# Eight experts on one core: the last two results in one tile, and one more weight tile loaded in halves

## The chip, the cores and the metric

The kernel runs on one core of a Trainium2 chip. The metric is the device time of one execution in microseconds (us), the median of three runs. The profile is that of one further execution; its span starts at the first and ends at the last recorded instruction, and is shorter than the device time by some 1.8 us.

## The reference

There are 8 experts. Each takes 256 tokens of width 512 through a hidden layer of width 2048 with ReLU and back. All inputs and the result are float32.

```python
# x (8,256,512)  w1 (8,512,2048)  w2 (8,2048,512)  b1 (8,2048)  b2 (8,512)
h = np.matmul(x, w1) + b1[:, np.newaxis, :]
h = np.maximum(h, 0)
out = (np.matmul(h, w2) + b2[:, np.newaxis, :]).astype(np.float32)
```

w1 and w2 of one expert are 4 MB each in float32, so 64 MB of weights are read for 4 MB of input and 4 MB of results.

## The kernel before

**Stages.** For every expert there are two products. The first (`first_product`, L114) makes hT, the hidden layer with the 2048 hidden units on partitions, in 16 blocks of 128 units (j), each of 4 matmuls over the input width (kc) followed by one ScalarE instruction that adds the bias, takes the ReLU and writes fp16 (L128). The second (`second_product`, L166) makes the result for two blocks of 128 tokens (tb) in the PSUM tiles po0 and po1: one matmul with a row of ones for the bias b2 (L171), then 16 matmuls over j (L178) for each tb. The inputs are turned by VectorE in 32x32 blocks (`transposes`, L95).

**Order.** The loop at L227 runs over steps s = 0 to 10. Step s does the first product of expert s and then the second product of expert s - 3 (LAG = 3), so steps 8, 9 and 10 have the second products of experts 5, 6 and 7 alone. Nearly all transfers are issued by GpSimd in an order written out by hand, the `ring` list (L215 to L225), and kept so by `ordered`. GpSimd's loads also turn float32 in memory into fp16 in the tile. The ring ends with w2 of expert 7, then the two flushes (L138), which store the results of the groups of experts. A load can be issued only when the buffer that it overwrites has been used up; w1 and w2 have three buffers each.

**w2 in halves.** `load_w2` (L88) loads the w2 of the experts in HALVED (6 and 7) as two transfers, j = 0 to 7 and j = 8 to 15. For these experts `second_product` does both token blocks with the first half of j and then both with the second (L174 to L177), so that it can start when half of the tile has landed. For the others po0 is finished before po1 is begun, and all of w2 is needed at the start.

**Results.** `store` (L142) copies po0 by VectorE (L156) and po1 by ScalarE (L157) to SBUF. Experts 0 to 3 share one tile and so do experts 4 and 5 (GROUPS, L36): with n experts to a tile, an expert takes 128 / n partitions, and a partition holds 2n consecutive tokens of one expert, which are 4n KB in one piece in the result. Each po tile is then copied in n pieces of 128 / n partitions. hT's tokens are put in a matching order by L128 (`split`). A group's tile is stored by its flush, on GpSimd's queue. Experts 6 and 7 are in no group: each has a tile of its own from out_pool with rows of 4 KB, stored at once by L164. Expert 6's goes out in three pieces (PARTS, L40): rows 0 to 24 and 121 to 127 by SyncE and rows 25 to 120 by ScalarE. Expert 7's goes out in one piece of 128 rows by SyncE.

Of the DMA queues in the profile, q0 is that of GpSimd's transfers, q1 that of SyncE's and q10 that of ScalarE's; q8 loads instructions.

Of the kernel before, what the change touches and what calls it, by code (L numbers as in the profile page):

```python
# [10 lines left out]
def kernel(  # L11
# [9 lines left out]
    nc = tc.nc  # L21
    fp32 = mybir.dt.float32
    fp16 = mybir.dt.float16
    E, T, H = x.shape
    M = w1.shape[2]
    P = 128
    nTB = T // P
# [4 lines left out]
    LAG = 3  # L32

    GROUPS = {0: 4, 4: 2}  # L36
    HALVED = (E - 2, E - 1)


    PARTS = {E - 2: ((0, 25, False), (25, 121, True), (121, 128, False))}  # L40
    nXF32 = 2
    X_LOADS = {2: 2, 4: 4}

    def ordered(ins):
        return tc.keep_in_program_order(ins)
# [7 lines left out]
    group_pool = ctx.enter_context(tc.tile_pool(name="groups", bufs=1))  # L53
    out_pool = ctx.enter_context(tc.tile_pool(name="outp", bufs=2))
# [13 lines left out]
    pending = {}  # L68
    results = {}
    group_of = {first + i: (first, n) for first, n in GROUPS.items() for i in range(n)}  # L70

# [16 lines left out]
    def load_w2(e):  # L88
        src = w2[e].rearrange("(p j) h -> p j h", j=nJ)
        w2_sb[e] = w2_pool.tile([P, nJ, H], fp16, tag="w2", name="w2sb")  # L90
        half = nJ // 2 if e in HALVED else nJ
        for lo in range(0, nJ, half):
            ordered(nc.gpsimd.dma_start(out=w2_sb[e][:, lo : lo + half], in_=src[:, lo : lo + half]))  # L93

    def transposes(e):  # L95


        t, p0, R = x16[e]
        n = R // nTB
        xT[e] = xT_pool.tile([P, nKC, T], fp16, tag="xT", name="xT")  # L100
        for g in range(T // R // B):
            src = t[p0 + B * g : p0 + B * (g + 1)]
            for b in range(nB):
                block = src[:, :, b * (H // nB) : (b + 1) * (H // nB)].rearrange(
                    "p (n tb) (i kc) -> p tb kc n i", tb=nTB, kc=nKC)
                out = xT[e][b * B : (b + 1) * B].rearrange(
                    "p kc (tb g i n) -> p tb g kc n i", tb=nTB, i=B, n=n)
                if n == 1:
                    nc.vector.transpose(out=out[:, :, g, :, 0, :], in_=block[:, :, :, 0, :])  # L109
                    continue  # L110
                for tb in range(nTB):
                    nc.vector.transpose(out=out[:, tb, g], in_=block[:, tb])  # L112

    def first_product(e):  # L114
        hT[e] = hT_pool.tile([P, nJ, T], fp16, tag="hT", name="hT")
        split = group_of[e][1] if e in group_of else 1
        for j in range(nJ):
            bias_at = j * B + e * nB + nB - 1
            ph = psum_h.tile([P, T], fp32, tag="ph", name="ph")
            for kc in range(nKC):  # L120
                ordered(nc.tensor.matmul(  # L121
                    out=ph,
                    lhsT=w1_sb[e][:, kc, :].rearrange("p (q j) -> p q j", j=nJ)[:, :, j],
                    rhs=xT[e][:, kc, :],
                    start=(kc == 0),
                    stop=(kc == nKC - 1),
                ))
            nc.scalar.activation(  # L128
                out=hT[e][:, j, :].rearrange("p (tb k i) -> p tb k i", tb=nTB, k=split),
                in_=ph.rearrange("p (tb i k) -> p tb k i", tb=nTB, k=split),  # L130
                func=mybir.ActivationFunctionType.Relu,
                bias=b1T[:, bias_at : bias_at + 1],
                scale=1.0,
            )
            if j == nJ // 2 and e + 1 < E:
                transposes(e + 1)
# [3 lines left out]
        ordered(nc.gpsimd.dma_start(out=dst, in_=src))  # L140

    def store(e, po):  # L142
        if e in group_of:
            first, n = group_of[e]
            split, rows = n, P // n
            if e == first:
                results[e] = group_pool.tile(
                    [P, split * nTB, H], fp32, tag=f"out{e}", name=f"out{e}")
        else:
            first, n, split, rows = e, 1, 1, P  # L150
            results[e] = out_pool.tile([P, nTB, H], fp32, tag="out", name="out")
        out_sb = results[first]
        at = (e - first) * rows
        for k in range(split):
            part = slice(k * rows, (k + 1) * rows)
            nc.vector.tensor_copy(out=out_sb[at : at + rows, k * nTB, :], in_=po[0][part])  # L156
            nc.scalar.copy(out=out_sb[at : at + rows, k * nTB + 1, :], in_=po[1][part])  # L157
        dst = out[first : first + n].rearrange("e (p r) h -> (e p) r h", r=split * nTB)
        if e in group_of:
            if e == first + n - 1:  # L160
                pending[first] = (dst, out_sb)
            return
        for p0, p1, scalar in PARTS.get(e, ((0, P, False),)):
            (nc.scalar if scalar else nc.sync).dma_start(out=dst[p0:p1], in_=out_sb[p0:p1])  # L164

    def second_product(e):  # L166
        po = []
        for tb in range(nTB):
            t = psum_o.tile([P, H], fp32, tag=f"po{tb}", name=f"po{tb}")
            po.append(t)  # L170
            ordered(nc.tensor.matmul(  # L171
                out=t, lhsT=ones1, rhs=b2_sb[0:1, e * H : (e + 1) * H], start=True, stop=False,
            ))
        half = nJ // 2 if e in HALVED else nJ  # L174
        for lo in range(0, nJ, half):
            for tb in range(nTB):
                for j in range(lo, lo + half):  # L177
                    ordered(nc.tensor.matmul(  # L178
                        out=po[tb],
                        lhsT=hT[e][:, j, tb * P : (tb + 1) * P],  # L180
                        rhs=w2_sb[e][:, j, :],
                        start=False,
                        stop=(j == nJ - 1),
                    ))
        store(e, po)

    x32 = []
    for e in range(nXF32):
# [4 lines left out]
        out=b2_sb,  # L193
        in_=b2.rearrange("e h -> (e h)").rearrange("(o f) -> o f", o=1),
# [12 lines left out]
    for b in range(nB):  # L207
        nc.vector.transpose(  # L208
            out=b1T[b * B : (b + 1) * B, nB - 1 - b : nB - 1 - b + nJ * B],
            in_=b1_rows.rearrange("r (i j) -> r j i", j=nJ),  # L210
# [4 lines left out]
    ring = []  # L215
# [6 lines left out]
            ring.append((s - 2, load_w2, (s - LAG,)))  # L222
    ring.append((E + LAG - 3, load_w2, (E - 1,)))
    for first, n in GROUPS.items():
        ring.append((first + n + LAG, flush, (first,)))  # L225

    for s in range(E + LAG):  # L227
        while ring and ring[0][0] <= s:
            _, put, args = ring.pop(0)
            put(*args)  # L230
        if s < E:
            first_product(s)
        if s >= LAG:
            second_product(s - LAG)
# [31 lines left out]
```

## Time and profile before

| what | value |
|---|---|
| device time | 181.51 us (181.47 to 181.75, 3 runs) |
| span of the profiled execution | 179.7 us |
| busy: PE, PEld, DVE, ACT, POOL | 129.1, 85.8, 88.0, 70.2, 13.1 us |
| DMA: GpSimd's queue (q0) | 3232 packets, 38.35 MB, 96.6% of 16 engines |
| DMA: SyncE's queue (q1) | 476 packets, 1.70 MB, 2.4% |
| DMA: ScalarE's queue (q10) | 112 packets, 0.39 MB, 0.5% |
| DMA: instructions (q8) | 6 packets, 0.10 MB, 0.2% |
| HBM | 71.39 MB read, 4.19 MB written |
| copy of a po tile, 64 or 128 partitions | DVE 0.69 us, ACT 0.58 to 0.59 us |
| half of w2 (1024 KB), issue to landing | 16.9 to 30.9 us |
| last store (512 KB), issue to landing | 4.8 us |

PE is the tensor engine's matmuls and PEld its weight loads, DVE is VectorE, ACT ScalarE and POOL GpSimd. In the slices each digit stands for a fortieth of the span, 4.5 us, in tenths. The queue's share is the summed time of its packets as a share of 16 DMA engines over the whole span; packets of one engine overlap a little, so shares can come out above 1 in a stretch. A transfer's time to landing runs from its issue, so for transfers that stand in a queue it is mostly waiting.

### The profile page before, as it was taken

Reading aid. Unit: us, or ns where it says so; the run is one execution under the profiler, and the core shown is the slowest. Engines: PE = TensorE matmul, PEld = TensorE weight load, DVE = VectorE, ACT = ScalarE, POOL = GpSimd, SP = SyncE. Lnnn points to the kernel's source line nnn. Section 1 sums busy time; section 2 is a strip of 40 time slices with the busy share of each in tenths; the row PEclk is TensorE's granted clock in tenths of the full one; section 3 lists DMA queues with packets and bytes.
Section 4 is the critical chain, followed back from the end, with each engine's and each line's share of the span. In section 5 each row is a group of like instructions: output and inputs, shape, how many; then the busy total and the mean of one; then the engine's idle time right before and its main releaser. Section 6 shows DMA issues by size and latency. Waiting matters only on the chain.

```text
span 179.7 us, 1958 instructions
## 1 busy us (share of the span) xinstructions
PE 129.1 (72%) x784; PEld 85.8 (48%) x784; DVE 88.0 (49%) x125; ACT 70.2 (39%) x151; POOL 13.1 (7%) x28
## 2 busy tenths in 40 slices
PE   0005099969595970899969597969497887999950
PEld 0004079969592320795369244844195332433420
DVE  0999942987000199999999998003200020301010
ACT  0000459969593022483099005950586020020010
POOL 7000002120201010001010001000200021010000
PEclk9999999999998798589999889999999996999996
DMA  5999999999999999999999999999999999999996
GB/s 216 251 226 199 233 212 197 233 224 193 228 230 192 221 233 215 197 230 230 204 208 230 219 193 233 226 193 222 230 215 197 233 206 204 223 212 215 335 420 250
DMA packets 3829, 40.56 MB, mean 226 GB/s; under 512 B 461, under 2 KB 477, under 8 KB 1133
## 3 DMA queue, kind: packets, MB, share of 16 engines
q0 software_dynamic: 3232, 38.35, 96.6%
q1 hardware_dynamic: 476, 1.70, 2.4%
q10 hardware_dynamic: 112, 0.39, 0.5%
q8 instruction: 6, 0.10, 0.2%
q14 instruction: 3, 0.02, 0.0%
HBM read 71.39 MB, written 4.19 MB: 421 GB/s over the span
## 4 chain that ended last, share of the span: by engine, by line
DMA 66%; PE 26%; POOL 2%; another core or an unknown queue 1%; issue 1%; ACT 0%; POOLq 0%
DMA w1sb<-in_w_dram 44%; DMA w2sb<-in_w_dram 22%; PE po L178 18%; PE ph L121 8%; PE po L171 1%; POOL w1sb L84 1%; ACT out L157 0%; POOL x L76 0%; POOL b_sb L192 0%; POOL b_rows L196 0%; POOLq L250 0%
## 5 line engine op out<-in xcount | busy, mean ns | idle before, releaser
L121 PE MATMUL ph<-xT,w1sb 128*128 128x256 f16 x512 | 63.6, 289 | 34.8 <-DMA w1sb<-in_w_dram 23.9
L121 PEld LDWEIGHTS <-w1sb 128*128 128x128 f16 x512 | 59.0, 147 | 40.3 <-DMA w1sb<-in_w_dram 32.6
L178 PE MATMUL po<-w2sb,hT 128*128 128x512 f16 x256 | 61.4, 402 | 9.4 <-DMA w2sb<-in_w_dram 9.4
L112 DVE STREAM_TRANSPOSE xT<-x 32x256 f16<-32x256 f16 (+1 forms) x64 | 53.1, 889 | 25.6 <-DMA x<-in_x_dram 18.7
L128 ACT ACTIVATE hT<-ph,b1T 128x256 f16<-128x256 f32 x128 | 56.2, 474 | 13.6 <-PE ph L121 13.4
L178 PEld LDWEIGHTS <-hT 128*128 128x128 f16 x256 | 25.9, 102 | 44.7 <-issue 19.3
L156 DVE COPY out<-po 32x512 f32<-32x512 f32 (+2 forms) x22 | 15.1, 688 | 54.0 <-PE po L178 53.8
L157 ACT COPY out<-po 32x512 f32<-32x512 f32 (+2 forms) x22 | 12.7, 579 | 69.7 <-PE po L178 69.5
L109 DVE STREAM_TRANSPOSE xT<-x 32x256 f16<-32x256 f16 x32 | 14.0, 436 | 0.5
L93 POOL DMA_DIRECT2D w2sb<-in_w_dram x10 | 5.3, 534 | 72.8 <-PE po L178 72.8
L128 ACT ACT_TABLE_LOAD x1 | 1.3, 1283 | 20.5 <-DVE b1T L208 20.5
L84 POOL DMA_DIRECT2D w1sb<-in_w_dram x8 | 4.5, 558 | 63.2 <-PE ph L121 62.4
L171 PE MATMUL po<-b_sb,ones 1*128 1x512 f16 x16 | 4.8, 379 | 0.0
L208 DVE STREAM_TRANSPOSE b1T<-b_rows 32x512 f32<-32x512 f32 x4 | 4.1, 1035 | 0.1
L201 DVE CAST x<-x 128x1024 f16<-128x1024 f32 x2 | 1.5, 757 | 3.3 <-DMA x<-in_x_dram 3.3
L140 POOL DMA_DIRECT2D out_dram<-out x2 | 1.1, 542 | 10.9 <-ACT out L157 10.9
L171 PEld LDWEIGHTS <-ones 1*128 1x128 f16 x16 | 0.9, 92 | 2.1 <-issue 2.1
L76 POOL DMA_DIRECT2D x<-in_x_dram x2 | 1.1, 552 | 0.0
L197 DVE MEMSET ones<- 1x128 f16 x1 | 0.2, 165 | 0.8 <-PEq L250 0.8
L196 POOL DMA_DIRECT2D b_rows<-in_b_dram x1 | 0.5, 515 | 0.0
L192 POOL DMA_DIRECT2D b_sb<-in_b_dram x1 | 0.5, 513 | 0.0
L250 POOL MEMSET const-float32-0.0<- 128x1 f32 x1 | 0.1, 99 | 0.2 <-issue 0.2
(3 smaller groups left out, 0.3 us busy)
## 6 DMA issues: line engine op xcount, KB each, us to landing
w1sb<-in_w_dram POOLq DMA_DIRECT2D x8, 2048.0 KB, 34.5
w2sb<-in_w_dram POOLq DMA_DIRECT2D x6, 2048.0 KB, 46.8
w2sb<-in_w_dram POOLq DMA_DIRECT2D x4, 1024.0 KB, 24.0
out_dram<-out POOLq DMA_DIRECT2D x1, 2048.0 KB, 26.8
x<-in_x_dram SPq DMA_DIRECT2D x2, 512.0 KB, 3.9
x<-in_x_dram POOLq DMA_DIRECT2D x1, 1024.0 KB, 30.8
out_dram<-out POOLq DMA_DIRECT2D x1, 1024.0 KB, 17.8
x<-in_x_dram POOLq DMA_DIRECT2D x1, 512.0 KB, 24.0
```

Source lines behind the costliest of these rows:

```text
L84: ordered(nc.gpsimd.dma_start(out=w1_sb[e], in_=w1[e].rearrange("(p kc) m -> p kc m", kc=nKC)))
L93: ordered(nc.gpsimd.dma_start(out=w2_sb[e][:, lo : lo + half], in_=src[:, lo : lo + half]))
L109: nc.vector.transpose(out=out[:, :, g, :, 0, :], in_=block[:, :, :, 0, :])
L112: nc.vector.transpose(out=out[:, tb, g], in_=block[:, tb])
L121: ordered(nc.tensor.matmul(out=ph, lhsT=w1_sb[e][:, kc, :].rearrange("p (q j) -> p q j", j=nJ)[:, :, j], rhs=xT[e][:, kc, :], start=(kc == 0),
L128: nc.scalar.activation(out=hT[e][:, j, :].rearrange("p (tb k i) -> p tb k i", tb=nTB, k=split), in_=ph.rearrange("p (tb i k) -> p tb k i", ...
L156: nc.vector.tensor_copy(out=out_sb[at : at + rows, k * nTB, :], in_=po[0][part])
L157: nc.scalar.copy(out=out_sb[at : at + rows, k * nTB + 1, :], in_=po[1][part])
L171: ordered(nc.tensor.matmul(out=t, lhsT=ones1, rhs=b2_sb[0:1, e * H : (e + 1) * H], start=True, stop=False,))
L178: ordered(nc.tensor.matmul(out=po[tb], lhsT=hT[e][:, j, tb * P : (tb + 1) * P], rhs=w2_sb[e][:, j, :], start=False, stop=(j == nJ - 1),))
L201: nc.vector.tensor_copy(out=t, in_=x32[e])
L208: nc.vector.transpose(out=b1T[b * B : (b + 1) * B, nB - 1 - b : nB - 1 - b + nJ * B], in_=b1_rows.rearrange("r (i j) -> r j i", j=nJ),)
```

## The change

Experts 6 and 7 become a group of two: their results share one tile, expert 6 on partitions 0 to 63 and expert 7 on 64 to 127, with 8 KB to a row, and nothing of it is stored before both are there. The tile is stored by four transfers after expert 7: rows 0 to 111 by SyncE, and rows 112 to 116, 117 to 121 and 122 to 127 by ScalarE. It isn't flushed by GpSimd. The store of expert 6 in three pieces goes away.

Each po tile of experts 6 and 7 is now copied in two pieces of 64 partitions. VectorE has both pieces of po0; ScalarE has both of po1, but for expert 7 the second one of po1 is given to VectorE, so that the last two copies can run side by side.

HALVED takes in expert 5: its w2 is loaded as two transfers, and its second product goes over the first half of j for both token blocks and then over the second, so that it can begin earlier.

All experts being in groups, the branches for an expert outside one are dropped.

```diff
-    GROUPS = {0: 4, 4: 2}
-    HALVED = (E - 2, E - 1)
-    PARTS = {E - 2: ((0, 25, False), (25, 121, True), (121, 128, False))}
+    GROUPS = {0: 4, 4: 2, 6: 2}
+    HALVED = (E - 3, E - 2, E - 1)
+    PARTS = ((0, 112, False), (112, 117, True), (117, 122, True), (122, 128, True))
...
     def first_product(e):
-        split = group_of[e][1] if e in group_of else 1
+        split = group_of[e][1]
...
     def store(e, po):
-        if e in group_of:
-            first, n = group_of[e]
-            split, rows = n, P // n
-            if e == first:
-                results[e] = group_pool.tile(
-                    [P, split * nTB, H], fp32, tag=f"out{e}", name=f"out{e}")
-        else:
-            first, n, split, rows = e, 1, 1, P
-            results[e] = out_pool.tile([P, nTB, H], fp32, tag="out", name="out")
+        first, n = group_of[e]
+        rows = P // n
+        if e == first:
+            results[e] = group_pool.tile([P, n * nTB, H], fp32, tag=f"out{e}", name=f"out{e}")
         out_sb = results[first]
         at = (e - first) * rows
-        for k in range(split):
-            part = slice(k * rows, (k + 1) * rows)
-            nc.vector.tensor_copy(out=out_sb[at : at + rows, k * nTB, :], in_=po[0][part])
-            nc.scalar.copy(out=out_sb[at : at + rows, k * nTB + 1, :], in_=po[1][part])
-        dst = out[first : first + n].rearrange("e (p r) h -> (e p) r h", r=split * nTB)
-        if e in group_of:
-            if e == first + n - 1:
-                pending[first] = (dst, out_sb)
+        for tb in range(nTB):
+            for k in range(n):
+                to = out_sb[at : at + rows, k * nTB + tb, :]
+                part = po[tb][k * rows : (k + 1) * rows]
+                if tb == 0 or (e == E - 1 and k > 0):
+                    nc.vector.tensor_copy(out=to, in_=part)
+                else:
+                    nc.scalar.copy(out=to, in_=part)
+        if e < first + n - 1:
             return
-        for p0, p1, scalar in PARTS.get(e, ((0, P, False),)):
+        dst = out[first : first + n].rearrange("e (p r) h -> (e p) r h", r=n * nTB)
+        if e < E - 1:
+            pending[first] = (dst, out_sb)
+            return
+        for p0, p1, scalar in PARTS:
             (nc.scalar if scalar else nc.sync).dma_start(out=dst[p0:p1], in_=out_sb[p0:p1])
...
     for first, n in GROUPS.items():
-        ring.append((first + n + LAG, flush, (first,)))
+        if first + n < E:
+            ring.append((first + n + LAG, flush, (first,)))
```

## The prediction, made before the changed kernel was run

> **What bounds the kernel now.** I read the page's slices first, then the chain, then the end of the run in windows, then the timeline.
>
> ```profile
> DMA  5999999999999999999999999999999999999996
> GB/s 216 251 226 199 233 212 197 233 224 193 228 230 192 221 233 215 197 230 230 204 208 230 219 193 233 226 193 222 230 215 197 233 206 204 223 212 215 335 420 250
> ...
> DMA 66%; PE 26%; POOL 2%; another core or an unknown queue 1%; issue 1%; ACT 0%; POOLq 0%
> ```
>
> The 16 DMA engines are busy from the first slice to the last. The rate nearly doubles in the last three slices because a load counts the fp16 bytes written (half of what is read) and a store counts all its bytes. All 4 MB of results leave there, behind the weights. The windows of the last 14 us show it finer (columns: window, length, busy time and count of PE, PEld, DVE, ACT, POOL, clock, DMA share, GB/s):
>
> ```profile
> 166.00:168.00 2.00, 2.00 (x11) 0.85 (x10) 0.00 (x0) 0.37 (x1) 0.00 (x0) 1.00 1.08 242
> ...
> 170.00:172.00 2.00, 2.00 (x11) 0.88 (x9) 0.39 (x1) 0.00 (x0) 0.00 (x0) 1.00 0.98 416
> ...
> 174.00:176.00 2.00, 0.00 (x0) 0.00 (x0) 0.00 (x0) 0.00 (x0) 0.00 (x0) 1.00 0.98 410
> 176.00:178.00 2.00, 0.00 (x0) 0.00 (x0) 0.00 (x0) 0.00 (x0) 0.00 (x0) 0.67 0.87 358
> 178.00:179.70 1.70, 0.00 (x0) 0.00 (x0) 0.00 (x0) 0.00 (x0) 0.00 (x0) 0.50 0.08 31
> ```
>
> No compute engine works after 173.9 us, yet the DMA share stays near 1 until about 177. The last store is not waiting for results; it stands in line. The timeline has its issue (start, length, engine, line, what, in brackets the idle time before and what ended it):
>
> ```profile
> 149.54 8.66 PE L178 MATMUL po<-w2sb,hT 128*128 128x512 f16 x32 [2.09 <-DMA w2sb<-in_w_dram]
> ...
> 158.67 7.08 PE L178 MATMUL po<-w2sb,hT 128*128 128x512 f16 x32
> ...
> 166.21 7.08 PE L178 MATMUL po<-w2sb,hT 128*128 128x512 f16 x32
> 166.40 7.91 SPq L164 DMA_DIRECT2D out_dram<-out  x3
> 166.40 0.38 ACTq L164 DMA_DIRECT2D out_dram<-out  x1
> 171.61 0.69 DVE L156 COPY out<-po 128x512 f32<-128x512 f32 x1 [6.85 <-PE po L178]
> 173.33 0.59 ACT L157 COPY out<-po 128x512 f32<-128x512 f32 x1 [6.96 <-PE po L178]
> ```
>
> Three second products (experts 5, 6, 7) run back to back; the first waits 2.09 us for w2 of expert 5 and then runs 8.66 us instead of 7.0, because the clock is 0.5 from 149.4 to 152.8. Expert 7's store is issued at 173.94. In the trace's records its first packet moves at 175.79, on an engine that had just finished the GpSimd queue, and its sixteen shares land in two groups: five at 177.40 to 177.90, eleven at 178.48 to 178.78. Their mean is 178.35. So the end is set by the summed DMA work and by its unevenness, 0.43 us.
>
> That unevenness has a visible source: the page counts 6 instruction packets of 16 KB, which took 0.89 to 0.97 us each. The shares of the last w2 half land as ten at 167.89 to 168.34 and six at 168.80 to 169.23: six engines run one such packet late.
>
> [...]the 25-row store has five landings (174.75 to 174.97) beside one jump at 166.87, the 7-row store seven. That the five are engines 0 to 4 no record shows;[...] from 170.2 us packets of ScalarE's queue alternate with the 16 KB ones of GpSimd's.[...] Here 3.41 us pieces at half clock followed windows in which PE was 43% to 47% busy, and none followed one at 50%.
>
> **The change part by part.**
>
> *Rows of 8 KB for experts 6 and 7.* Packets took 159 ns for 4 KB and 309 ns for 8 KB (the first group's 16 KB: 613). Before, engines 0 to 4 carry 5 + 1 rows of the two small SyncE stores, 6 of the ScalarE store and 8 of expert 7: 20 x 0.159 = 3.18 us. The other engines carry 14 (or 15): 2.23 us. After, 112 rows give each engine 7;[...] engines 0 to 4 have 10, engine 5 has 8, the rest 7: 3.09 and 2.16 us. That is -0.09 on engines 0 to 4 and -0.06 on the late engines (none of which can be among 0 to 4: extra rows and lateness would have added up to a landing near 179.6). The three extra rows, 0.93 us, fill the same engines as the old extra rows (6 x 0.159 = 0.95).
>
> *w2 of expert 5 in halves.* A whole tile is eight 16 KB packets an engine at 1,227 ns, the halves sixteen of 8 KB at 625 ns: +0.18 us by durations. But packets overlap (the DMA share reads up to 1.06), so I take landings: w2 of expert 5, whole, landed 9.69 us after its forerunner (139.81 to 149.50); expert 6's two halves took 9.76 (149.50 to 159.26). Bounds +0.07 and +0.18, value +0.1, on every engine: this is on the path. One more GpSimd issue, 0.53 us, is free: GpSimd is busy 7% and issues w2 of expert 5 at 110.1, almost 30 us before its data move.
>
> *What the halves do to PE.* The first half lands about 144.7, before expert 4's product ends (139.85 + 7.07 = 146.9). So expert 5 follows at once: 146.9 + 0.53 (bias pair) + 7.0 = 154.5, without the 2.09 us wait and, with that window no longer half idle, without the half clock. Then PE meets the loads. Half products take 3.5 us; the loads land at 154.4, 159.3, 164.1 and 169.2 (issue plus time to landing), each +0.1. Expert 6: 155.0 to 158.5, wait, 159.4 to 162.9. Expert 7: waits to 164.2, to 167.7, waits to 169.35, ends 172.9 instead of 173.31. The new waits hold up only these products and the copies behind them. Of 3.7 us gained at expert 5, some 0.4 is left at the end.
>
> *Copies.* Expert 7's halves of 64 partitions cost as much each as a whole one (DVE 688 ns, ACT 580, from the 64x512 rows of the groups by form). DVE has two for po0, about 171.1 to 172.5, beside PE. Of po1 ACT and DVE take one each, so 0.69 us follows PE in place of 0.59. The issue moves from 173.94 to about 173.65. Expert 6's extra copies lie beside PE. The three small ScalarE issues, 0.38 us each, wait for the DVE copy; nothing else is behind them, and their rows stand behind seven rows of 0.309 us on each engine, so these issues are hidden too.
>
> *The store of expert 6 waits for expert 7.* This moves 512 KB from among the other stores to behind them. Where the line stays full, that costs nothing. Is it full? Engines 0 to 4 finish the GpSimd queue between 176.7 and 177.2 now; without twelve 4 KB packets (1.9 us) and with +0.1 that is 174.9 to 175.4. The final store's first packet comes 1.03 us after issue at the least (the first x load: issued 0.74, moving 1.77) and 1.85 at the most (expert 7 before): 174.7 to 175.5. So idle time is 0 to 0.6 us; I take 0.05, since the middle of both intervals is alike. The flush of experts 4 and 5 is issued some 4 us earlier, behind the same queue: nothing.
>
> *Sum.* On engines 0 to 4: -0.09 + 0.1 + 0.05 = +0.06; on the late ones, which are busy with the GpSimd queue to about 176: -0.06 + 0.1 = +0.04. Add 0.06 to 181.51: **181.6 us**, no change that can be told.
>
> **The rivals.**
>
> *No change (0.50).* As worked out, between 181.15 and 181.87. For it: the DMA share, and that neither edit changes how many bytes move.
>
> *Slower: the line runs dry (0.20).* If the last store's latency is at its upper bound, or the halves cost the full 0.18, engines 0 to 4 end 0.4 to 0.7 us later: 181.9 to 182.2. For it: expert 6's store, issued at 166.40, moved only at 170.2.[...]
>
> *Slower: PE at half clock (0.09).* PE now waits near its end, up to 1.65 us in one 3.41 us window: 52% busy, just above the 50% that still kept the clock. If it halves at about 169.9, the last half product takes some 1.7 us more, the store comes at 175.3 and finds engines idle for 1.3 us: about 182.9.
>
> *Faster (0.21).* If the shares came out even, the landing would be the mean, 178.35 in place of 178.78, and the longer rows would give 0.05 more: 181.05 at best. For it: five engines are done 0.6 to 1.4 us early. Against: the new rows leave the same engines empty.
>
> **How the numbers follow.** The likeliest case gives 181.6. The range takes in the dry line (182.3) and nearly all of the faster case (181.1); it leaves out half clock and the outer edges, about 2 in 10. Chances: faster 0.21, same 0.50, slower 0.29 (0.20 + 0.09).
>
> **What would show it.** Right: expert 5's product in about 7.0 us with no DMA wait, three short waits of PE after it, the SyncE issue near 173.65, no GpSimd packets after about 176.5, landings again in two groups with the last near 178.8, DMA share near 1 until 177. Wrong: a window between 174 and 177 with a share well under 1 (dry line), a clock of 0.5 about 170 us, last landings spread evenly (faster), or instruction packets on engines 0 to 4.

## The result and the profile after

The changed kernel takes 183.64 us (183.36 to 183.89, 5 runs) against 181.71 us for the kernel before beside it: ratio 1.011, 95% interval 1.0095 to 1.0124. It is slower by about 2 us. The forecast was 181.6 us, no change that can be told, with a range up to 182.3.

First the windows of the end, as shown of the kernel before (window, length, busy time and count of PE, PEld, DVE, ACT, POOL, clock, DMA share, GB/s), now of the changed kernel:

```profile
166.00:168.00 2.00, 1.83 (x9) 0.73 (x8) 0.00 (x0) 0.00 (x0) 0.00 (x0) 1.00 1.00 225
170.00:172.00 2.00, 2.00 (x11) 0.93 (x10) 0.54 (x1) 0.00 (x0) 0.00 (x0) 1.00 0.95 410
174.00:176.00 2.00, 0.00 (x0) 0.00 (x0) 0.49 (x1) 0.00 (x0) 0.00 (x0) 1.00 1.00 373
176.00:178.00 2.00, 0.00 (x0) 0.00 (x0) 0.00 (x0) 0.00 (x0) 0.00 (x0) 0.70 0.93 340
178.00:180.00 2.00, 0.00 (x0) 0.00 (x0) 0.00 (x0) 0.00 (x0) 0.00 (x0) 0.50 0.34 123
180.00:181.80 1.80, 0.00 (x0) 0.00 (x0) 0.00 (x0) 0.00 (x0) 0.00 (x0) 0.50 0.02 9
```

Up to 172 the rates differ little. There is no dry line: the DMA share is 1.00 from 174 to 176. But look at the rate beside it, 373 GB/s in place of 410: engines that count as busy move less. And the share is still 0.34 between 178 and 180, where the kernel before had all but done (0.08): a few engines work on alone.

The timeline of the changed kernel says what they work on (start, length, engine, line, what, in brackets the idle time before and what ended it):

```profile
147.42 7.08 PE L178 MATMUL po<-w2sb,hT 128*128 128x512 f16 x32
...
159.35 3.61 PE L178 MATMUL po<-w2sb,hT 128*128 128x512 f16 x16 [0.76 <-DMA w2sb<-in_w_dram]
...
164.22 3.61 PE L178 MATMUL po<-w2sb,hT 128*128 128x512 f16 x16 [0.72 <-DMA w2sb<-in_w_dram]
...
169.54 3.61 PE L178 MATMUL po<-w2sb,hT 128*128 128x512 f16 x16 [1.71 <-DMA w2sb<-in_w_dram]
...
173.19 0.58 ACT L156 COPY out<-po 64x512 f32<-64x512 f32 x1 [9.01 <-PE po L178]
173.80 0.69 DVE L154 COPY out<-po 64x512 f32<-64x512 f32 x1 [0.94 <-ACT out L156]
174.52 0.36 SPq L164 DMA_DIRECT2D out_dram<-out  x1
174.53 3.38 ACTq L164 DMA_DIRECT2D out_dram<-out  x3
```

PE does what the halves were for: expert 5's product follows at once, and then three short waits eat the gain, at full clock. The last two copies do not run side by side: VectorE waits for ScalarE, so the stores are issued at 174.52. And the three ScalarE issues take 3.38 us together; the trace has them at 0.57, 1.02 and 1.72 us, so the last is out at 177.9. In its landing records (16 for the SyncE store of 112 rows; 5, 5 and 6, beside one jump each, for the ScalarE pieces) the SyncE store lands from 178.19 to 180.36, the third ScalarE piece from 179.36 to 180.98. Before, the last landing was at 178.78.

Which engines carry the pieces ("engines 0 to 4 have 10" in the prediction, "the five lowest engines" in what was expected of runs) was the author's assumption; no record names an engine. What the landings show is that twice SyncE's store, the second and the third piece land in steps of one row's time: at 179.72, 180.04 and 180.34, and at 180.36, 180.68 and 180.98. That looks like one engine with a share of each.

The packets of the last stores are long. The DMA view of the changed kernel from 175.0 to 181.8 (queue, packets, MB, share of 16 engines):

```profile
q1 hardware_dynamic: 128, 0.92, 36.6%
q10 hardware_dynamic: 32, 0.13, 8.6%
```

ScalarE's 16 rows took 8.6% of 16 x 6.8 us, 9.4 us: 0.58 us a row in place of 0.309. SyncE's 112 rows took 39.8 us in place of 34.6. In sum the rows were **9.4 us longer** than 309 ns each by the packet records (the kernel before: 0.6). I call this sum the excess. For rows of 4 KB it is counted against 309 ns for two of them, though one takes 159 ns by itself: 0.6 us for 128 such rows, or 1.2 us for 256, means that none was lengthened.

### The profile page after: what moved, and what is told of

Read it like the earlier page. It is cut to its first block, busy times and chain, and to the rows that moved or that the text cites. A ratio compares the mean times of both kernels' runs of the same rounds, so it can differ in the third digit from the quotient of the medians.

```text
span 181.9 us, 1957 instructions
## 1 busy us (share of the span) xinstructions
PE 128.1 (70%) x784; PEld 85.6 (47%) x784; DVE 89.9 (49%) x128; ACT 70.8 (39%) x152; POOL 13.9 (8%) x29
## 4 chain that ended last, share of the span: by engine, by line
DMA 58%; PE 20%; DVE 14%; issue 2%; ACT 1%; POOL 1%; DVEq 0%; ACTq 0%
DMA w2sb<-in_w_dram 39%; DMA x<-in_x_dram 19%; PE ph L121 10%; PE po L178 10%; DVE xT L109 6%; DVE xT L112 5%; DVE b1T L208 2%; DVE x L201 1%; ACT L128 1%; POOL w2sb L93 0%; DVE out L154 0%; ACT out L156 0%; PE po L171 0%; POOL w1sb L84 0%; ACT hT L128 0%
## 5 line engine op out<-in xcount | busy, mean ns | idle before, releaser
L121 PE MATMUL ph<-xT,w1sb 128*128 128x256 f16 x512 | 63.9, 290 | 34.6 <-DMA w1sb<-in_w_dram 24.0
L121 PEld LDWEIGHTS <-w1sb 128*128 128x128 f16 x512 | 59.2, 147 | 40.2 <-DMA w1sb<-in_w_dram 32.6
L178 PE MATMUL po<-w2sb,hT 128*128 128x512 f16 x256 | 60.2, 394 | 10.4 <-DMA w2sb<-in_w_dram 10.4
L154 DVE COPY out<-po 32x512 f32<-32x512 f32 (+1 forms) x25 | 17.2, 688 | 54.2 <-PE po L178 53.0
L156 ACT COPY out<-po 32x512 f32<-32x512 f32 (+1 forms) x23 | 13.3, 579 | 68.9 <-PE po L178 68.7
L93 POOL DMA_DIRECT2D w2sb<-in_w_dram x11 | 5.8, 534 | 72.2 <-PE po L178 72.2
## 6 DMA issues: line engine op xcount, KB each, us to landing
w1sb<-in_w_dram POOLq DMA_DIRECT2D x8, 2048.0 KB, 34.6
```

The lines of the kernel that those rows point to most:

```text
L121: ordered(nc.tensor.matmul(out=ph, lhsT=w1_sb[e][:, kc, :].rearrange("p (q j) -> p q j", j=nJ)[:, :, j], rhs=xT[e][:, kc, :], start=(kc == 0),
L154: nc.vector.tensor_copy(out=to, in_=part)
L156: nc.scalar.copy(out=to, in_=part)
L178: ordered(nc.tensor.matmul(out=po[tb], lhsT=hT[e][:, j, tb * P : (tb + 1) * P], rhs=w2_sb[e][:, j, :], start=False, stop=(j == nJ - 1),))
```

## The experiments

Each kernel ran beside the kernel before on the same chip; the ratios are to it.

| kernel | us | ratio, 95% interval | excess, us | last landing, us |
|---|---|---|---|---|
| the changed kernel | 183.64 | 1.011 (1.0095 to 1.0124) | 9.4 | 180.98 |
| one store of 128 rows | 181.78 | 1.0004 (0.9995 to 1.0013) | 0.6 | 179.19 |
| 112 + 16 rows, the 16 by ScalarE | 183.06 | 1.0078 (1.0054 to 1.0101) | 11.4 | 180.03 |
| before, w2 of expert 5 in halves | 181.84 | 1.0004 (0.9992 to 1.0015) | 0.7 | 178.98 |
| before, expert 7's store in pieces | 182.39 | 1.004 (1.0026 to 1.0053) | 3.8 | 179.30 |
| two stores by columns | 181.94 | 1.0016 (1.0006 to 1.0027) | 1.2 | 179.13 |
| 112 + 16 rows, both by SyncE | 182.05 | 1.0024 (1.0014 to 1.0034) | 8.8 | 179.98 |
| 112 rows alone | 181.85 | 1.0008 (0.9996 to 1.0021) | 5.4 | 179.54 |
| 80 + 3 x 16 rows | 182.60 | 1.0053 (1.0038 to 1.0067) | 10.9 | 179.94 |
| 112 + 4 x 4 neighbouring rows | 183.91 | 1.0114 (1.009 to 1.0137) | 9.7 | 181.31 |
| 112 + 4 x 4 rows 4 apart | 183.11 | 1.0073 (1.0047 to 1.0099) | 6.9 | 180.16 |
| 112, 5, 5, 6 rows, all by SyncE | 182.78 | 1.0056 (1.0038 to 1.0074) | 9.3 | 180.33 |
| one store, w2 of expert 5 whole | 181.98 | 1.0013 (0.9995 to 1.0031) | 0.6 | 179.47 |
| near partitions to far rows | 183.92 | 1.0121 (1.0081 to 1.0161) | 9.7 | 181.22 |
| far partitions to near rows | 183.31 | 1.0081 (1.0042 to 1.0119) | 8.1 | 180.46 |
| before, expert 6's store in pieces | 181.84 | 1.0002 (0.9985 to 1.002) | 0.6 | 179.42 |

Excess and landing are of the one profiled run; where the rows are split, single runs differ by more than 1 us (112 + 16 by SyncE: 181.73 to 183.03), so the ratios carry the argument and the profile the mechanism. The profiled run isn't always near the median: with 112 + 16 rows by SyncE it took 182.65 us, with 16 by ScalarE 182.69, with 112 rows alone 182.19. The excess doesn't put the kernels in the order of their times either: 8.8 us go with a ratio of 1.0024, 9.4 with 1.011.

In the diffs below, replaced lines that have been shown before are left out, and so is a loop header that takes one name more.

**Which part of the change costs.** Four runs undo one part or do one part alone.

The joint tile leaves in one store:

```diff
-    PARTS = ((0, 112, False), (112, 117, True), (117, 122, True), (122, 128, True))
+    PARTS = ((0, 128, False),)
```

> The changed kernel, but the tile of experts 6 and 7 leaves in one SyncE store of 128 rows, so that every DMA engine has 8 rows of 8 KB and ScalarE issues no store. If the small pieces end the kernel (pieces theory): most of the 1.9 us comes back, about 182.2 us, with the last landing near 179.3 us; what stays over the kernel before (0.5 us) is the later issue, 174.5 in place of 173.9 us. If the late issue and the joint store are the cause (copies theory): 183.2 to 183.7 us. If the halves of w2 are the cause: no change, 183.6 us.

It is the kernel before again, 1.0004, a little better than the pieces theory asked. The windows of this run:

```profile
174.00:176.00 2.00, 0.00 (x0) 0.00 (x0) 0.43 (x1) 0.00 (x0) 0.00 (x0) 1.00 0.93 393
176.00:178.00 2.00, 0.00 (x0) 0.00 (x0) 0.00 (x0) 0.00 (x0) 0.00 (x0) 0.85 0.92 381
178.00:180.00 2.00, 0.00 (x0) 0.00 (x0) 0.00 (x0) 0.00 (x0) 0.00 (x0) 0.50 0.09 37
```

The share between 178 and 180 is 0.09 in place of 0.34. Its timeline has the same late end of the copies:

```profile
173.74 0.69 DVE L154 COPY out<-po 64x512 f32<-64x512 f32 x1 [0.94 <-ACT out L156]
174.46 0.35 SPq L164 DMA_DIRECT2D out_dram<-out  x1
```

So the joint tile, its copies and an issue half a microsecond later cost nothing that can be measured. The copies theory falls.

A piece of 16 rows, meant as one to each engine, in place of 5, 5 and 6:

```diff
-    PARTS = ((0, 112, False), (112, 117, True), (117, 122, True), (122, 128, True))
+    PARTS = ((0, 112, False), (112, 128, True))
```

> The changed kernel with rows 112 to 127 in one ScalarE store of 16 rows (one row on each of 16 engines) in place of the pieces of 5, 5 and 6. Pieces theory: if it is the extra rows on the five lowest engines and the three issues one after the other that cost, this is as good as one store, about 182.2 us; if any short second store on ScalarE's queue costs, it stays near 183.5 us. Copies theory: 183.5 us.

None of the numbers named was met: 183.06. With one row on each of 16 engines none has more than another here (both stores on SyncE's queue, further below, make 160 packets: 128 rows and 16 small ones for each store). Only one ScalarE store is issued (0.40 us), and two thirds of the loss remain. So neither the extra rows on five engines nor the issues one after the other are the main thing.

The halves alone, and the pieces alone, on the kernel before:

```diff
-    HALVED = (E - 2, E - 1)
+    HALVED = (E - 3, E - 2, E - 1)
```

> The kernel before with w2 of expert 5 in halves and nothing else. Pieces theory and copies theory: no change beyond the smaller packets, 181.6 to 181.8 us, with the product of expert 5 at 7.0 us and no wait. If the halves are the cause (PE's waits near the end): about 183.5 us.

```diff
-    PARTS = {E - 2: ((0, 25, False), (25, 121, True), (121, 128, False))}
+    PARTS = {E - 2: ((0, 25, False), (25, 121, True), (121, 128, False)),
+             E - 1: ((0, 112, False), (112, 117, True), (117, 122, True), (122, 128, True))}
```

> The kernel before with one edit: expert 7's own tile (4 KB rows) leaves as 112 rows by SyncE and 5, 5 and 6 rows by ScalarE, in place of 128 rows by SyncE. Pieces theory: slower than before by 0.9 us or more, 182.5 to 183.5 us, with long ScalarE issues and the last landing on ScalarE's queue. Copies theory: within 0.5 us of before, 181.6 to 182.0 us, from the extra rows on engines 0 to 4 alone (3 x 0.16 us).

The halves cost nothing. The pieces alone cost 0.4%, just short of the band named. Of the signs named, the long ScalarE issues came (0.51, 1.03 and 1.96 us); the last landing, at 179.30, was SyncE's, with ScalarE's at 179.26. With 8 KB rows the same pieces cost 1.0% over one store; that store holds twice the bytes, so the length of a row and the size of the store are not told apart. The halves' run shows one thing more:

```profile
163.54 12.49 SPq L164 DMA_DIRECT2D out_dram<-out  x3
...
169.72 5.30 PE L178 MATMUL po<-w2sb,hT 128*128 128x512 f16 x16 [1.96 <-DMA w2sb<-in_w_dram]
```

After a wait of 1.96 us the clock fell to half from 170.65 on, the last half product took 5.30 us in place of 3.61, and the last store was issued only at 175.67. That was a rival of the prediction. Here, where expert 6 still leaves early and the line is full to 177, it cost nothing (1.0004).

**Rows or queues.** Two explanations of the long packets were left: that rows are shared out otherwise than 8 to an engine (rows theory), or that two hardware queues have work at one moment (queues theory). Four runs tell them apart.

```diff
-    PARTS = ((0, 112, False), (112, 117, True), (117, 122, True), (122, 128, True))
+    PARTS = ((0, 2, False), (2, 4, True))
...
-            (nc.scalar if scalar else nc.sync).dma_start(out=dst[p0:p1], in_=out_sb[p0:p1])
+            (nc.scalar if scalar else nc.sync).dma_start(out=dst[:, p0:p1], in_=out_sb[:, p0:p1])
```

> The changed kernel with its last tile stored by columns: all 128 rows of its first 4 KB by SyncE and of its last 4 KB by ScalarE, so that two hardware queues run at once but each DMA engine has the same 8 rows in both, as in one store of 128 rows. Measured beside the time: by how much the packets of the last stores are longer in sum than 309 ns for 8 KB (9.4 us in the changed kernel, 11.4 us with 112 + 16 rows on two queues, 0.6 us with one store). Rows theory[...]: excess under 1.5 us, time 181.6 to 182.0 us. Queues theory (two hardware queues with work at the same moment lengthen each other's packets): excess 4 us or more, time 182.6 to 183.2 us.

```diff
+    PARTS = ((0, 112, False), (112, 128, False))
```

> The changed kernel with 112 and 16 rows as two stores, both by SyncE. Rows theory: the packets are longer in sum by 4 us or more and the time is 182.4 to 183.2 us, as with the 16 rows on ScalarE's queue (183.06). Queues theory: excess under 1.5 us, time 181.7 to 182.0 us.

```diff
+    PARTS = ((0, 112, False),)
```

> The changed kernel with the 112-row SyncE store alone; rows 112 to 127 of the last tile (the last 64 tokens of expert 7) are not stored, so each DMA engine has 7 rows in place of 8. Rows theory: the packets of the 112 rows are longer by 3 us or more in sum, and the last landing is not earlier than with one store of 128 rows (179.2 us) although an eighth less is stored; time 181.6 to 182.3 us. Queues theory: no excess, landing 0.3 us earlier than with 128 rows, time 181.3 to 181.6 us.

```diff
+    PARTS = ((0, 80, False), (80, 96, True), (96, 112, True), (112, 128, True))
```

> The changed kernel with 80 rows by SyncE and three ScalarE stores of 16 rows (one row to each of the 16 engines). It asks what makes the three ScalarE issues long (0.57, 1.02, 1.73 us in the changed kernel): if it is the small engine count (5, 5, 6 of 16) or the load on the lowest engines, the issues take about 0.4 us each; if it is the third store in a row on a queue, they grow as before. Rows theory: 80 rows are 5 to an engine, so the packets are long again, excess 4 us or more, time 182.5 to 183.5 us. Queues theory: the same time.

With two queues and 128 rows each, packets keep their length (excess 1.2, all 4 KB packets at 156 to 166 ns). With one queue and 112 + 16 rows they do not (8.8). And 112 rows alone take as much packet time as 128. Here are SyncE's queue from 175.0 to 180.0 in the run with one store of 128 rows and then in that with 112 rows alone:

```profile
q1 hardware_dynamic: 144, 1.05, 50.3%
```

```profile
q1 hardware_dynamic: 128, 0.92, 50.1%
```

Of 16 x 5 us that is 40.2 us for 1.05 MB and 40.1 us for 0.92 MB; the smaller store landed 0.35 us later, at 179.54, in a run 0.34 us above its median; by the ratios the two are equal (1.0004 and 1.0008). In the first three runs the packets speak for the rows theory; for the fourth both theories had named the same. The queues theory falls as the whole cause, since packets are long with one queue too. On the times both were too coarse: 112 + 16 rows on one queue cost 1.0024, under the band of the rows theory, against 1.0078 with the 16 on ScalarE's queue. So a second queue makes split rows dearer. The store by columns doesn't show that a second queue is harmless as such: its ScalarE part was issued 0.73 us after SyncE's, and its packets moved only from 176.07 on, as the first engines were done with SyncE's. With 112 + 16 rows both queues' packets moved from 175.4 and 176.0 on. The three ScalarE issues of the fourth run took 0.40, 0.44 and 1.76 us. So it is not the small engine count alone; the third in a row is long again.

**Near or apart, SBUF or memory.** If engines meet at rows that are neighbours, rows 4 apart should be free of it. In what was expected this guess is called the port theory.

```diff
+    PARTS = ((0, 112, False), (112, 116, True), (116, 120, True), (120, 124, True), (124, 128, True))
```

> The changed kernel with rows 112 to 127 in four ScalarE stores of 4 neighbouring rows each (112 to 115, and so on), 112 rows by SyncE as before. Pair with the next run, in which the same four engines carry the same number of rows from partitions that lie 4 apart. Port theory[...]: the four packets of the first piece take about 4 x 0.309 = 1.2 us each or a little less, and ScalarE's 16 packets are longer in sum by 2.5 us or more. Without ports (lengthening comes from a short store as such): the same excess in both runs of the pair. Time 183.3 to 184.3 us, as lengthening issues on ScalarE and 4 extra rows on four engines add up.

```diff
+    PARTS = ((0, 112, 1, False), (112, 125, 4, True), (113, 126, 4, True), (114, 127, 4, True), (115, 128, 4, True))
...
+            (nc.scalar if scalar else nc.sync).dma_start(out=dst[p0:p1:step], in_=out_sb[p0:p1:step])
```

> The changed kernel with rows 112 to 127 in four ScalarE stores of 4 rows that lie 4 apart (112, 116, 120, 124, and so on). Port theory: the four packets of the first piece[...] take 0.3 to 0.65 us each, ScalarE's 16 packets are longer in sum by 1.5 us at the most, and the kernel is a little faster than with neighbouring rows (by 0.1 to 0.5 us), the issues and the extra rows being the same. Without ports: no difference between the two.

Neighbouring rows and memory rows were then crossed, since rows that are neighbours in partitions are so in the result too. The near case:

```diff
+    NEAR = [slice(0, 112)] + [slice(112 + 4 * i, 116 + 4 * i) for i in range(4)]
+    APART = [slice(0, 112)] + [slice(112 + i, 125 + i, 4) for i in range(4)]
...
+        for i, (to, rows) in enumerate(zip(APART, NEAR)):
+            (nc.scalar if i else nc.sync).dma_start(out=dst[to], in_=out_sb[rows])
```

> As the four pieces of 4 rows, but crossed: each ScalarE store reads 4 neighbouring partitions (112 to 115, and so on) and writes them to rows of the result that lie 4 apart, so the last 16 rows of the result are in another order. If the engines meet on the SBUF side (port theory): the first piece's packets take about 1.2 us each as with neighbouring rows on both sides, ScalarE's packets are longer in sum by 2.5 us or more, 183.6 to 184.1 us. If they meet on the memory side: no ScalarE packet is longer, 182.8 to 183.3 us.

The far case has `zip(NEAR, APART)` in the third line:

> The cross the other way: each ScalarE store reads partitions 4 apart (112, 116, 120, 124, and so on) and writes them to 4 neighbouring rows of the result, so the last 16 rows are in another order. Port theory: no ScalarE packet is longer, 182.8 to 183.3 us, as with rows 4 apart on both sides. Memory side: the first piece's packets take about 1.2 us each, 183.6 to 184.1 us.

ScalarE's queue over 0.8 us, from the first packet of its rows, in these four runs in the order of the text:

```profile
q10 hardware_dynamic: 4, 0.03, 39.5%
```

```profile
q10 hardware_dynamic: 16, 0.08, 24.6%
```

```profile
q10 hardware_dynamic: 4, 0.03, 48.1%
```

```profile
q10 hardware_dynamic: 16, 0.08, 24.6%
```

Of 16 x 0.8 us, four near rows took 5.1 us (1.17 to 1.47 us each) and, crossed, 6.2 us (1.24 to 2.13 each). Rows apart: ten rows in 3.1 us, 0.31 each, with four moving at once, and the same crossed. The kernel with rows apart was 0.8 us faster, more than the 0.1 to 0.5 us named. In these four runs the length goes with the partitions read and not with the place in memory: 1.24 to 2.13 us from near partitions into far rows, 0.31 from far partitions into near rows. So the engines seem to meet on the SBUF side. If four of them shared what one has alone, a row would take 4 x 0.309 = 1.24 us: an estimate, near the 1.17 to 1.47 measured. What they would share, no run shows. One reserve: with rows apart ScalarE's first row moved only at 178.4, when most of SyncE's had gone, so SyncE's rows were not in the way as they were at 175.3 with near rows. The later pieces help here, since near rows moved late too. First ScalarE's queue with near partitions and far rows from 179.1 to 180.0, then with rows 4 apart from 178.3 to 179.6:

```profile
q10 hardware_dynamic: 10, 0.05, 18.1%
```

```profile
q10 hardware_dynamic: 28, 0.13, 24.3%
```

Of 16 x 0.9 us, six near rows took 2.6 us, 0.43 each and up to 0.70, beside two rows of SyncE's; of 16 x 1.3 us, all 16 rows apart took 5.0 us, 0.31 each. That SyncE's 112 rows are long for the same reason is argued from this: no run moved them to other partitions. The kernels with rows apart still take 183.11 and 183.31, as SyncE's 112 rows keep their excess (6.9 and 8.1 us) and the four pieces come behind them.

**Place in the queue.** The kernel before has pieces too (25, 96, 7), and its packets are not long. Expert 6's store there, in the new pieces:

```diff
-    PARTS = {E - 2: ((0, 25, False), (25, 121, True), (121, 128, False))}
+    PARTS = {E - 2: ((0, 112, False), (112, 117, True), (117, 122, True), (122, 128, True))}
```

> The kernel before with expert 6's store, which stands in the middle of the queue, in pieces of 112, 5, 5 and 6 rows in place of 25, 96 and 7. If it is their place at the end that makes such pieces dear (the engines have nothing else to work on meanwhile, and nothing hides a late issue): packets of 159 ns as before, 181.5 to 181.8 us. If it is their shape: packets longer in sum by 2 us or more, as where expert 7's store is cut so (3.8 us), and 181.9 to 182.6 us.

No change, 1.0002, and none of those 128 packets took over 162 ns. The same pieces are harmless in the middle of the queue and dear at the end. In the middle packets of three queues are mixed: in the kernel before, from 170.2 to 172.2 us, 40 of ScalarE's queue, 16 of SyncE's and 37 of GpSimd's. That this is what spreads the pieces is argued, not shown.

**What is left of the pieces.** All four on SyncE:

```diff
+    PARTS = ((0, 112, False), (112, 117, False), (117, 122, False), (122, 128, False))
```

> The changed kernel with all four pieces (112, 5, 5, 6) issued by SyncE[...]. If two hardware queues at work at once are what makes the pieces dear (16 rows on ScalarE's queue cost 183.06, on SyncE's 182.05 us): 182.2 to 182.8 us, and the issues one after the other grow as on ScalarE. If the five lowest engines and their extra rows are: 183.4 us or more.

182.78, at the edge of the first band. Its issues take 0.36, 0.51, 1.24 and 1.32 us, so long issues are not ScalarE's own. With this the loss can be set out in steps by ratio: one store 1.0004, the rows split 112 + 16 on one queue 1.0024, the 16 in 5, 5 and 6 1.0056, those by ScalarE 1.011. The last step, about 1.0 us, is half of the loss, and 112 + 16 rows show it too (1.0024 to 1.0078). It is shown as a cost; how it comes about is not.

Last, the halves beside the joint tile:

```diff
-    HALVED = (E - 3, E - 2, E - 1)
-    PARTS = ((0, 112, False), (112, 117, True), (117, 122, True), (122, 128, True))
+    HALVED = (E - 2, E - 1)
+    PARTS = ((0, 128, False),)
```

> The joint tile in one SyncE store of 128 rows, and w2 of expert 5 whole as in the kernel before. It asks what the halves are worth beside the joint tile (with them 181.78 us). PE then ends at about 173.3 in place of 173.1 us and the issue comes at 174.6 or 174.7, the line being dry a little longer, but the larger w2 packets give back about 0.1 us: 181.7 to 182.0 us. If the halves are needed to keep the line full: 182.1 us or more.

1.0013 with an interval that holds 1, so the halves' worth stays under what can be told. The issue came at 174.67, as expected.

No version beat the kernel before. The six late engines, up to 0.9 us behind in the joint tile's single store (landings 178.15 to 178.32 and 178.68 to 179.19), would be the thing to even out.

## Why the prediction was wrong

**What bounds the kernel** was read rightly: DMA work and its unevenness at the end. GpSimd's queue ended at 176.48 (forecast 176.5). The landings in two groups with the last near 178.8 came with one store (178.15 to 178.32 and 178.68 to 179.19), but not in the changed kernel, where they run on to 180.98.

**The step that failed** is "Rows of 8 KB for experts 6 and 7": it gave every row 0.309 us whoever reads it, so that engines 0 to 4 had "3.09" us for ten rows. That price came from stores of 128 rows, whose packets keep their length (excess 0.6 us). 112 rows in 16 shares are 7 to an engine, and the runs show such rows taking longer: 112 alone had 5.4 us of excess and the packet time of 128. In the changed kernel the first ScalarE piece did worse; its five rows from 175.3 to 175.9:

```profile
q10 hardware_dynamic: 5, 0.04, 50.0%
```

Of 16 x 0.6 us that is 4.8 us, and four of the five rows took 0.9 to 1.2 us each in place of 0.309. All five rows of that piece began between 175.35 and 175.89, and the last row of all ended at 180.64. If one engine had its ten rows between, as the prediction counts them, these took 4.7 to 5.3 us, with what GpSimd's queue still had for it, in place of 3.09: an estimate, since the records don't tell the engines apart. The three extra rows "fill the same engines as the old extra rows" in the prediction's count, but not in place: the old ones stood in the middle of the queue, where the new pieces cost nothing (1.0002). How much of the 1.9 us each part has is known from the ratios alone: about 0.4 us for rows split on one queue, 0.6 us for 5, 5 and 6 in place of 16, 1.0 us for ScalarE's queue, whose mechanism stays open.

**"So these issues are hidden too"** held in the changed kernel, though the price was wrong. The issues were priced 0.38 us each from a single one; one after the other they took 0.57, 1.02 and 1.72 us. But the second was over at 176.15, and its first row moved at 178.40, behind SyncE's rows as forecast. By the packet records each of the eleven rows of the second and third pieces starts 2 to 3 ns after another row ends; the last two, at 180.02 and 180.33, follow SyncE's last row, which began at 179.69 and took 0.33 us. The records don't name the engines, but so late few other packets are left. There is no sign of an engine that waited for an issue.

**Copies.** "Of po1 ACT and DVE take one each, so 0.69 us follows PE": they ran one after the other, with a wait of 0.94 us, and the issue came at 174.52 in place of 173.65. ScalarE read partitions 0 to 63 of po1 and VectorE 64 to 127. Whether the wait comes from po1, which both read, or from the joint tile, which both write, no run here shows. It cost nothing (one store: 1.0004). SyncE's first packet of the last store moved at 175.39, inside the forecast 174.7 to 175.5, but by luck: the issue was 0.87 us late, and the packet came 0.87 us after it, sooner than the "1.03 us after issue at the least".

**The halves.** Right: 7.08 us without a wait, waits of 0.76, 0.72 and 1.71 us, full clock in the changed kernel, and no cost (1.0004 alone). What they gave was lost in these waits, as forecast. But "just above the 50% that still kept the clock" was no safe ground. In the changed kernel the window from 166.58 to 169.99 was 50% busy, and the clock held. In the run with one store and w2 of expert 5 whole the window from 118.39 to 121.81 was 57% busy (1.94 us), and half clock followed. In the run with the halves alone that from 44.36 to 47.77 was 43% busy (1.47 us), and full clock followed. The busy share of one window doesn't decide it, so that the clock held was luck. The share of DMA "up to 1.06" is a smaller slip: a line of the same text has 1.08.

**The rivals.** None of the three was it. The dry line did not happen (DMA share 1.00 from 174 to 176), nor half clock near the end in the changed kernel. The slower side was argued from the wrong resource, so the range stopped at 182.3. Without the pieces the forecast of no change was right (one store: 1.0004), and the cost of pieces at the end, about 1.9 us by that run, was missing from the sum.

## What to carry to other kernels

A store's cost is not its rows times the price of a row: at the end of a kernel, where nothing else is queued, compare the share of the queue and the rate in its windows; a share near 1 at a lower rate, for transfers of the same kind, means that packets take longer than before (here 1.00 at 373 GB/s, where the kernel before had 0.98 at 410). Here the last store was best left one transfer of all 128 partitions, and uneven pieces did no harm in the middle of a full queue (1.0002). Price several issues in a row from several in a row, and look for what their rows wait for before blaming the issues.

## What the hardware showed that was not expected

- Four packets that moved at one moment took 1.17 to 1.47 us for 8 KB each from neighbouring partitions, and 0.309 us from partitions 4 apart, there when most of SyncE's rows had gone.
- 112 rows alone took as much packet time as 128 (40.1 and 40.2 us), and the kernel was no faster without the other 16 rows (1.0008 and 1.0004).
- Store issues one behind the other grow: 0.57, 1.02, 1.72 us on ScalarE for 5, 5, 6 rows; 0.40, 0.44, 1.76 us for 16 rows each; 0.51, 1.24, 1.32 us on SyncE. Why stays open; no run took it apart.
- On a second queue split rows cost more than on one: 1.0078 against 1.0024 for the same 112 + 16 rows, though two queues with whole 128-row stores cost 1.0016, there with one queue's packets behind the other's. This too stays open.
